# One 512-column matmul for both activation parts in the FFN and output products of a two-layer trunk

## The chip, the core and the metric

The kernel runs on one core of a Trainium2 chip. Its time is the device time of one execution in microseconds (us); the median of three runs is the figure to be predicted.

## What is computed

The reference is a two-layer decoder trunk over 256 tokens of width 2048. What matters here is the second half of each layer and the product that ends the first half:

```python
mod = cond @ ada_w[l] + ada_b[l]                 # 6 vectors of 2048: shift, scale, gate, twice
h = rms_norm(x, norm_mix[l]) * (1.0 + sc1) + sh1
x = x + g1 * hybrid_mixer(h, ...)                # four head groups, concatenated, then y @ w_o
h = rms_norm(x, norm_ffn[l]) * (1.0 + sc2) + sh2
u = causal_dwconv(h @ w_up, conv_w, conv_b)      # width 3; w_up is 2048 x 11264
a, g = split(u); x = x + g2 * ((silu(g) * a) @ w_down)   # w_down is 5632 x 2048
```

All of it is in float32, and the products keep that precision by splitting.

## The kernel before

The sequence lies on the free axis: an activation is a tile of 128 partitions (channels) by 256 tokens, a weight tile of 128x128 is the stationary operand, and a product sums 16 (or more) such tiles into PSUM. Float32 products are made of fast ones: every weight chunk is loaded as float32 (`raw`, 128x1024, 512 KB, `load_w`), ScalarE (ACT) casts it to `hi` (L217), VectorE (DVE) subtracts to get `lo` (L219), and the activations are kept as a pair `act[:, 0]` (high part) and `act[:, 1]` (rest), side by side in SBUF. `products` then gives three matmuls of 256 columns for each weight tile: hi x high, hi x rest, lo x high. The fourth is too small to matter. `raw` has four buffers, `hi` and `lo` three each, so the casts run at most two chunks ahead of TensorE (PE).

`gemm_t` is the product of the FFN and of the output projection. It takes 8 output tiles at a time: a chunk holds one k (128 input channels) and 8 output tiles, and two output tiles share one PSUM bank of 512 float32 columns. The output projection `wo` (L1056 to L1064) runs in two groups of 8 tiles and adds into x (L1061). Its PSUM pool has four banks under the tag `gp`, and `S` (two), `T` and `O` for the attention that runs just before. The last head group, the stick-breaking attention `sb_attn`, computes its eight heads while matmuls of `wo` that need only the other three groups are already possible. The order of instructions on each engine is fixed when the kernel is built, by a scheduler that works from priorities and its own costs.

The FFN works through 44 column tiles of each half of `w_up`: `up(g)` makes 4 of each half at once (11 groups), applies the width-3 convolution (one ACT and two DVE instructions for each tile, L1096 to L1100), SiLU, product and split. `down` multiplies what six (then five) such groups made with `w_down` and adds into x (L1118). The FFN's pool has all eight banks under `gp`. Ahead of it `norm_chunk` makes the 16 activation pairs of h: for each, a DVE multiply (L338), an ACT add (L342) and a DVE subtraction (L343).

The adaLN modulation has a weight matrix of 201 MB in the two layers. It isn't done on PE: a DMA brings 128x1024 pieces (`adaw`, three buffers) and DVE multiplies and sums each (L159, called a dot below, 384 of them). The dots are spread over the program: `tick` adds `rate[0]` to a credit at every weight chunk, and each whole credit emits one job of two dots at a low priority. `RATE[l][i]` sets the rate by layer and phase; phases 3 and 4 are the FFN before and after its first slab.

Of the kernel before, what the change touches and what calls it, by code (L numbers as in the profile page):

```python
# [61 lines left out]
RATE = ((0.45, 0.9, 0.45, 0.45, 0.22), (0.2, 0.2, 0.2, 0.1, 0.1))  # L62
# [10 lines left out]
def tile_trunk(ctx: ExitStack, tc: tile.TileContext, io, out, L):  # L73
# [159 lines left out]
    def gemm_t(pp, chunks, acts, G, tag="gp"):  # L233
# [19 lines left out]
        return ps  # L253

# [739 lines left out]
    for l in range(L):  # L994
# [75 lines left out]
        with ExitStack() as s2:  # L1070
# [14 lines left out]
            def up(g):  # L1085
                ps = gemm_t(pp, [io["wup"][l, g, k] for k in range(KD)], h, 8)
                res = []
                for p in range(2):
                    uu = []
                    for half in range(2):  # L1090
                        src = ps[2 * half + p]
                        u = fp.tile([P, 2, T], F32, tag=f"u{half}", name="u", bufs=2)
                        for q in range(2):
                            i = half * NFF + g * 4 + p * 2 + q
                            w0, w1, w2 = (fw[:, j * 2 * NFF + i:j * 2 * NFF + i + 1] for j in range(3))
                            nc.scalar.activation(u[:, q, :], src[:, q, :], AF.Identity, scale=w2, bias=fb[:, i:i + 1])  # L1096
                            nc.vector.scalar_tensor_tensor(  # L1097
                                u[:, q, 1:], src[:, q, :T - 1], w1, u[:, q, 1:], op0=ALU.mult, op1=ALU.add
                            )
                            nc.vector.scalar_tensor_tensor(  # L1100
                                u[:, q, 2:], src[:, q, :T - 2], w0, u[:, q, 2:], op0=ALU.mult, op1=ALU.add
                            )
                        uu.append(u)
                    sg = fp.tile([P, 2, T], F32, tag="sg", name="sg", bufs=2)
                    last_silu[0] = nc.scalar.activation(sg, uu[1], AF.Silu)
                    nc.vector.tensor_mul(uu[0], uu[0], sg)
                    y_ = fp.tile([P, 2, 2, T], F32R, tag="g", name="g", bufs=14)
                    split(y_, uu[0])
                    res += [y_[:, 0], y_[:, 1]]
                return res  # L1110

            def down(k0, acts, st=None):
                for mg in range(2):
                    ps = gemm_t(pp, [io["wdn"][l, k0 + k, mg] for k in range(len(acts))], acts, 8)
                    for m in range(8):
                        c = mg * 8 + m
                        g2 = mod(l, 5, c | 3)
                        nc.vector.scalar_tensor_tensor(  # L1118
                            x[:, c, :], ps[m // 2][:, m % 2, :], g2[:, c:c + 1], x[:, c, :],
                            op0=ALU.mult, op1=ALU.add,  # L1120
                        )
# [7 lines left out]
            NG = NFF // 4  # L1129
            for g in range(NG):  # L1130
# [4 lines left out]
                if g in (5, NG - 1):  # L1135
# [153 lines left out]
```

## Time and profile before

| | |
|---|---|
| median of 3 runs | 2481.59 us (2481.56 to 2487.34) |
| the profiled execution's own time | 2479.15 us |
| its span in the trace | 2476.8 us |
| PE busy, PE weight loads busy | 97%, 94% of the span |
| DVE busy, ACT busy | 75%, 47% of the span |
| mean granted clock of TensorE | 0.992 |

Busy shares are means over the whole span. Matmuls are pipelined, so the duration of one is longer than the distance from its start to the start of the next, and the latter is what a stream of them costs. In a timeline a row with "x2" is two instructions merged, in brackets stands how long the engine idled just before and what it waited for.

### The profile page before, as it was taken

To read this page: it belongs to the slowest core of one execution; us is meant where nothing else is said; L and a number is where in the kernel's file an instruction comes from. 1 tells how busy PE (TensorE), PEld (TensorE's weight loads), DVE (VectorE), ACT (ScalarE), POOL (GpSimd) and SP (SyncE) were. 2 spreads that over 40 slices of the span, in tenths; PEclk is the share of its full clock that TensorE was granted. 3 is DMA by queue.
4 is the path that set the end of the run, shared out by engine and by line. 5 is a ranking of instruction groups with operands and counts; after the bars stand their busy time and mean duration, and the time that the engine had idled before them with its cause. 6 is when DMAs were issued, how large, how long until landed. Compare 5 with 4: busy or idle time off the path is not lost.

```text
span 2476.8 us, 46041 instructions
## 1 busy us (share of the span) xinstructions
PE 2413.6 (97%) x18720; PEld 2330.1 (94%) x18720; DVE 1853.5 (75%) x2972; ACT 1165.0 (47%) x1704; POOL 24.0 (1%) x40
## 2 busy tenths in 40 slices
PE   7888999999999999999999999999999999999999
PEld 5666999989999999999999999999999999999999
DVE  6779988898888887888767997657676676455554
ACT  2124566445545433445444576644454453344442
POOL 0000000000000000000001000000000000000000
PEclk9999999999999999999999999999999999999999
DMA  8975778988888899888875574366666666655554
GB/s 319 347 256 190 252 271 274 336 300 295 282 307 296 290 331 325 312 304 293 290 259 181 181 242 162 128 222 213 221 207 233 230 207 222 187 176 191 184 182 162
DMA packets 169125, 610.31 MB, mean 246 GB/s; under 512 B 19025, under 2 KB 20945, under 8 KB 168401
## 3 DMA queue, kind: packets, MB, share of 16 engines
q1 hardware_dynamic: 168914, 607.39, 71.1%
q8 instruction: 146, 2.39, 0.4%
q14 instruction: 65, 0.53, 0.1%
HBM read 603.12 MB, written 4.19 MB: 245 GB/s over the span
## 4 chain that ended last, share of the span: by engine, by line
PE 85%; DVE 8%; DMA 4%; ACT 2%; issue 1%; SPq 0%; DVEq 0%; ACTq 0%
PE gt L245 71%; DMA adaw<-in_ada_dram 4%; DVE acc L565 3%; PE gt L359 2%; DVE adaw L159 2%; PE pv L266 2%; PE pn L266 1%; PE s L509 1%; PE po L535 1%; PE pq L266 1%; DVE lo L219 1%; PE tp L530 1%; PE ss L326 1%; ACT hi L217 0%; PE po L981 0%
## 5 line engine op out<-in xcount | busy, mean ns | idle before, releaser
L245 PE MATMUL gt<-act,hi 128*128 128x256 f32 x7232 | 1318.4, 284 | 4.3 <-ACT act L342 4.1
L217 ACT CAST hi<-raw 128x1024 fp32r<-128x1024 f32 (+3 forms) x716 | 739.5, 1033 | 1002.3 <-PE gt L245 831.7
L219 DVE TENSOR_TENSOR lo<-raw,hi 128x1024 fp32r<-128x1024 f32 (+3 forms) x716 | 859.1, 1203 | 388.4 <-ACT hi L217 386.6
L245 PEld LDWEIGHTS gt<-act,hi 128*128 128x128 f32 x7232 | 1129.5, 192 | 7.0 <-ACT act L342 4.9
L245 PE MATMUL gt<-act,lo 128*128 128x256 f32 x3616 | 1021.7, 285 | 3.5 <-DVE lo L219 3.4
L245 PEld LDWEIGHTS gt<-act,lo 128*128 128x128 f32 x3616 | 691.9, 192 | 4.9 <-DVE lo L219 4.7
L159 DVE SCALAR_TENSOR_TENSOR adaw<-adaw,cond 128x1024 f32<-128x1024 f32 x384 | 467.0, 1221 | 126.4 <-DMA adaw<-in_ada_dram 124.3
L245 PE MATMUL gt<-g,hi 128*128 128x256 f32 x2816 | 507.1, 283 | 0.0
L245 PEld LDWEIGHTS gt<-g,hi 128*128 128x128 f32 x2816 | 438.7, 192 | 0.2
L245 PE MATMUL gt<-g,lo 128*128 128x256 f32 x1408 | 396.9, 283 | 0.1
L245 PEld LDWEIGHTS gt<-g,lo 128*128 128x128 f32 x1408 | 269.5, 192 | 0.3 <-DVE lo L219 0.3
L359 PE MATMUL gt<-actw,raw 128*128 128x256 f32 x416 | 106.1, 418 | 26.4 <-ACT actw L340 26.4
L359 PEld LDWEIGHTS gt<-actw,raw 128*128 128x128 f32 x416 | 86.5, 211 | 45.9 <-ACT actw L340 32.3
L565 DVE SCALAR_TENSOR_TENSOR acc<-ug,vec,acc 128x256 f32<-128x256 f32 x240 | 98.9, 476 | 0.0
L1096 ACT ACTIVATE u<-gt,vec 128x256 f32<-128x256 f32 x176 | 94.2, 561 | 5.9 <-PE gt L245 3.4
L1097 DVE SCALAR_TENSOR_TENSOR u<-gt,vec,u 128x255 f32<-128x255 f32 x176 | 79.9, 474 | 3.2 <-ACT u L1096 3.2
L1100 DVE SCALAR_TENSOR_TENSOR u<-gt,vec,u 128x254 f32<-128x254 f32 x176 | 79.4, 472 | 0.0
L359 PE MATMUL gt<-act,hi 128*128 128x256 f32 x416 | 77.1, 287 | 2.1 <-ACT act L342 2.1
L359 PEld LDWEIGHTS gt<-act,hi 128*128 128x128 f32 x416 | 66.1, 195 | 2.5 <-ACT act L342 2.5
L340 ACT ACTIVATE actw<-t,sh 128x256 f32<-128x256 f32 x16 | 8.1, 507 | 121.8 <-DVE sh L414 121.3
L359 PE MATMUL gt<-act,lo 128*128 128x256 f32 x208 | 59.5, 286 | 0.0
L523 ACT ACTIVATE pt<-s,mx,scl 128x128 f32<-128x128 f32 (+1 forms) x96 | 48.4, 512 | 9.7 <-DVE mx L520 9.7
(284 smaller groups left out, 1786.2 us busy)
## 6 DMA issues: line engine op xcount, KB each, us to landing
adaw<-in_ada_dram SPq DMA_DIRECT2D x384, 512.0 KB, 5.5
raw<-in_wup_dram SPq DMA_DIRECT2D x352, 512.0 KB, 4.3
raw<-in_wdn_dram SPq DMA_DIRECT2D x176, 512.0 KB, 4.3
raw<-in_wo_dram SPq DMA_DIRECT2D x64, 512.0 KB, 4.7
raw<-in_wconv_dram SPq DMA_DIRECT2D x32, 512.0 KB, 5.5
raw<-in_wsqk_dram SPq DMA_DIRECT2D x32, 512.0 KB, 4.3
raw<-in_wlq_dram SPq DMA_DIRECT2D x32, 448.0 KB, 4.7
raw<-in_wnkv_dram SPq DMA_DIRECT2D x32, 412.0 KB, 3.1
```

The source lines that it names most:

```text
L159: nc.vector.scalar_tensor_tensor(w, w, 1.0, cond[:, hf * 1024:hf * 1024 + 1024], op0=ALU.mult, op1=ALU.mult, accum_out=raw[:, hf, j:j + 1],)
L217: nc.scalar.copy(hi[:, :n], raw[:, :n])
L219: nc.vector.tensor_sub(lo[:, :n], raw[:, :n], hi[:, :n].bitcast(F32))
L245: nc.tensor.matmul(ps[m // 2][:, m % 2, :], ww[:, c], x, start=(k == 0 and i == 0 and m % 2 == 0), stop=(k == K - 1 and i == len(prods) - ...
L266: nc.tensor.matmul(o, x[:, tt * P:(tt + 1) * P], ww[:, kk * N + c0:kk * N + c1], start=(k == 0 and i == 0 and first), stop=(k == K - 1 and ...
L326: nc.tensor.matmul(self.ss[:, 0, :], ones, sq[:, q, :], start=(self.n == 2 and q == 0), stop=(self.n == KD and q == 1 - join))
L359: nc.tensor.matmul(ps[m // 2][:, m % 2, :], ww[:, m * P:(m + 1) * P], xx, start=(first and i == 0 and m % 2 == 0), stop=(last and i == len ...
L523: nc.scalar.activation(pt[:, j, :n], s[:, j, :n], AF.Exp, scale=sc2[:, j:j + 1], bias=mx[:, j:j + 1], accum_out=rs[:, tt, 2 * pr + j:2 * p ...
L565: nc.vector.scalar_tensor_tensor(acc[:, c, :], ug[:, c, j:j + T], w, acc[:, c, :], op0=ALU.mult, op1=ALU.add)
L1096: nc.scalar.activation(u[:, q, :], src[:, q, :], AF.Identity, scale=w2, bias=fb[:, i:i + 1])
L1097: nc.vector.scalar_tensor_tensor(u[:, q, 1:], src[:, q, :T - 1], w1, u[:, q, 1:], op0=ALU.mult, op1=ALU.add)
L1100: nc.vector.scalar_tensor_tensor(u[:, q, 2:], src[:, q, :T - 2], w0, u[:, q, 2:], op0=ALU.mult, op1=ALU.add)
```

## The change

- A new `gemm_2` takes 4 output tiles at a time, each with a whole bank. For each k and tile it issues two matmuls: `hi` against both activation parts in one matmul of 512 columns (high part into the bank's first half, rest into its second), and `lo` against the high part, 256 columns, added into the second half. The three products that are summed stay the same.
- The halves of a bank are summed later. In `up` an ACT copy takes the second half to SBUF (`v`) and a DVE addition adds the first. In `down` and `wo` the multiply-add into x is done twice, once for each half.
- A chunk holds two k by 4 tiles instead of one k by 8. The number and size of the loads stay. `up` runs 22 groups instead of 11, `down` and `wo` 4 groups of output tiles instead of 2; in `wo` every second group takes the banks O, T, S and one gp.
- The FFN's rates of dots are now 0.2 in `up` and 0.42 in `down` in layer 0 (0.45 before and 0.22 after the first slab), 0.1 in both in layer 1 (as before).

```diff
-RATE = ((0.45, 0.9, 0.45, 0.45, 0.22), (0.2, 0.2, 0.2, 0.1, 0.1))
+RATE = ((0.45, 0.9, 0.45), (0.2, 0.2, 0.2))
+RATE_FFN = ((0.2, 0.42), (0.1, 0.1))
+    def gemm_2(banks, chunks, acts):
+        K, G = len(acts), len(banks)
+        k = 0
+        for src in chunks:
+            hi, lo = load_w(src)
+            for kk in range(src.shape[-1] // (G * P)):
+                x2 = acts[k].rearrange("p a t -> p (a t)")
+                for m in range(G):
+                    c = slice((kk * G + m) * P, (kk * G + m + 1) * P)
+                    nc.tensor.matmul(
+                        banks[m].rearrange("p a t -> p (a t)"), hi[:, c], x2,
+                        start=(k == 0), stop=False, skip_group_check=True,
+                    )
+                    nc.tensor.matmul(
+                        banks[m][:, 1, :], lo[:, c], acts[k][:, 0, :],
+                        start=False, stop=(k == K - 1), skip_group_check=True,
+                    )
+                k += 1
...
-        for mg in range(2):
-            ps = gemm_t(pp, [io["wo"][l, mg, k] for k in range(KD)], y, 8)
-            for m in range(8):
-                c = mg * 8 + m
+        for mg in range(4):
+            ps = [pp.tile([P, 2, T], F32, tag=t, name="gt") for t in (("gp",) * 4 if mg % 2 == 0 else ("O", "T", "S", "gp"))]
+            gemm_2(ps, [io["wo"][l, mg, k] for k in range(KD // 2)], y)
+            for m in range(4):
+                c = mg * 4 + m
                 g1 = mod(l, 2, c | 3)
-                nc.vector.scalar_tensor_tensor(
-                    x[:, c, :], ps[m // 2][:, m % 2, :], g1[:, c:c + 1], x[:, c, :], op0=ALU.mult, op1=ALU.add
-                )
+                for q in range(2):
+                    nc.vector.scalar_tensor_tensor(
+                        x[:, c, :], ps[m][:, q, :], g1[:, c:c + 1], x[:, c, :], op0=ALU.mult, op1=ALU.add
+                    )
...
+                        v = fp.tile([P, T], F32, tag="v", name="v", bufs=2)
+                        nc.scalar.copy(v, src[:, 1, :])
+                        nc.vector.tensor_add(v, src[:, 0, :], v)
```

The scheduler places everything anew. Three places matter below.

**TensorE at the end of the attention of layer 0.** `po` is the attention's output, `ss` sums the squares for the norm of this last head group, act_3463 is its first normed activation tile, and `gt` are the products of `wo`. Before:

```order
L982 MATMUL po_3381<-sa_3446,sv_2834 128x128
L245 MATMUL gt_3480<-act_3305,hi_3722 128x256 x2
...
L445 MATMUL ss_3453<-sq_3451,ones_73 128x256 x4
L245 MATMUL gt_3478<-act_3273,hi_3752 128x256 x2
L245 MATMUL gt_3478<-act_3273,lo_3754 128x256
L245 MATMUL gt_3479<-act_3273,hi_3752 128x256 x2
...
L245 MATMUL gt_3478<-act_3463,hi_3884 128x256 x2
```

Now:

```order
L1002 MATMUL z_3433<-ssp_3441,con_69 128x128
L1003 MATMUL z_3433<-ssp_3441,negones_75 128x128
L1006 MATMUL po_3381<-sa_3446,sv_2834 128x256
L1007 MATMUL po_3381<-sa_3446,sv_2834 128x128
L269 MATMUL gt_3702<-act_1553,hi_3708 128x512
L273 MATMUL gt_3702<-act_1553,lo_3710 128x256
L269 MATMUL gt_3702<-act_1553,hi_3708 128x512
L273 MATMUL gt_3702<-act_1553,lo_3710 128x256
L470 MATMUL ss_3453<-sq_3451,ones_73 128x256 x4
L269 MATMUL gt_3478<-act_3463,hi_3638 128x512
```

Before, 15 `gt` matmuls stood between `po` and `ss`, and 93 between `ss` and the first that reads act_3463 (165 in layer 1). Now four stand between `po` and `ss`, none behind `ss` (five and three in layer 1), and none between the last z and its `po`.

**VectorE at the start of the FFN of layer 1.** t1 and act are the two steps of `norm_chunk`, `lo` is a weight chunk's rest. Before, each further `lo` stood after two more chunks of h, and a chunk of weights served one k:

```order
L219 TENSOR_TENSOR lo_18692<-raw_18688,hi_18690 128x1024
L338 SCALAR_TENSOR_TENSOR t1_18557<-x_17469,amul_18547,actw_18536 128x256
...
L159 SCALAR_TENSOR_TENSOR adaw_18810,modr1_5_18290<-adaw_18810,cond_85 128x1024
...
L219 TENSOR_TENSOR lo_18722<-raw_18718,hi_18720 128x1024
L343 SCALAR_TENSOR_TENSOR act_18551<-t1_18582,mod1_3_11213,act_18551 128x256
```

Here lo_18692 is the third `lo` of the FFN and lo_18722 the fourth. Now:

```order
L222 TENSOR_TENSOR lo_16420<-raw_16416,hi_16418 128x1024
L368 SCALAR_TENSOR_TENSOR act_16274<-t1_16283,mod1_3_11155,act_16274 128x256
...
L363 SCALAR_TENSOR_TENSOR t1_16295<-x_15429,amul_16273,actw_16262 128x256
L161 SCALAR_TENSOR_TENSOR adaw_16357,modr1_4_11152<-adaw_16357,cond_85 128x1024
L368 SCALAR_TENSOR_TENSOR act_16275<-t1_16291,mod1_3_11155,act_16275 128x256
...
L363 SCALAR_TENSOR_TENSOR t1_16329<-x_15429,amul_16273,actw_16262 128x256
L1105 SCALAR_TENSOR_TENSOR amul_16273<-mod1_4_11154,vs1_7429 128x4
L178 TENSOR_TENSOR mod1_3_11155<-modr1_3_11153 128x4
L222 TENSOR_TENSOR lo_16442<-raw_16438,hi_16440 128x1024
L368 SCALAR_TENSOR_TENSOR act_16279<-t1_16325,mod1_3_11155,act_16279 128x256
```

lo_16420 is the second `lo` of this FFN (k = 2 and 3) and lo_16442 the third (k = 4 and 5). It stands behind the first ten chunks of h, with a dot in each of the four pairs of chunks after the first.

**VectorE at the start of the FFN of layer 0.** Before, the fourth `lo` stood behind the sixth chunk of h:

```order
L159 SCALAR_TENSOR_TENSOR adaw_4405,modr0_4_2227<-adaw_4405,cond_85 128x1024
L343 SCALAR_TENSOR_TENSOR act_4600<-t1_4624,mod0_3_2230,act_4600 128x256
...
L338 SCALAR_TENSOR_TENSOR t1_4636<-x_3475,amul_4597,actw_4586 128x256
L219 TENSOR_TENSOR lo_4814<-raw_4810,hi_4812 128x1024
```

Now the fourth, lo_4552 (k = 6 and 7), stands behind twelve chunks with one dot in each pair, and two more dots (three stand ahead of the fifth):

```order
L161 SCALAR_TENSOR_TENSOR adaw_4437,modr0_4_2227<-adaw_4437,cond_85 128x1024
L368 SCALAR_TENSOR_TENSOR act_4371<-t1_4417,mod0_3_2230,act_4371 128x256
L368 SCALAR_TENSOR_TENSOR act_4371<-t1_4421,mod0_3_2230,act_4371 128x256
L161 SCALAR_TENSOR_TENSOR adaw_4440,modr0_4_2227<-adaw_4440,cond_85 128x1024
L161 SCALAR_TENSOR_TENSOR adaw_4446,modr0_3_2228<-adaw_4446,cond_85 128x1024
L178 TENSOR_TENSOR mod0_4_2229<-modr0_4_2227 128x4
L222 TENSOR_TENSOR lo_4552<-raw_4548,hi_4550 128x1024
```

Over the program 143 of the 384 `adaw` loads were issued ahead of the FFN of layer 0 (now 145), 176 within it (now 156: 55 in the first 104 loads of `up`, 35 in the first `down`, 34 in the rest of `up`, 32 in the last `down`, which had 23), and 28 in the FFN of layer 1 (now 41).

## Rows read from the trace of the kernel before

**Rows 1.** The page: the span, and the engines' busy time.

```profile
span 2476.8 us, 46041 instructions
PE 2413.6 (97%) x18720; PEld 2330.1 (94%) x18720; DVE 1853.5 (75%) x2972; ACT 1165.0 (47%) x1704; POOL 24.0 (1%) x40
```

**Rows 2.** Busy time by stretch: in layer 0 the FFN's first seven groups of `up`, the rest of `up`, and the last `down`; in layer 1 the first `down`. Columns are the stretch, its length, busy time (instructions) of PE, weight loads, DVE, ACT and POOL, granted clock, DMA share, GB/s.

```profile
520.00:842.00 322.00, 319.89 (x2652) 319.48 (x2651) 276.74 (x416) 159.08 (x196) 0.00 (x0) 0.99 0.84 294
990.00:1174.00 184.00, 184.00 (x1536) 184.00 (x1535) 155.77 (x228) 89.59 (x108) 0.00 (x0) 1.00 0.86 304
1174.00:1290.00 116.00, 114.32 (x930) 112.85 (x929) 86.13 (x122) 49.30 (x55) 0.20 (x1) 1.00 0.79 279
2032.00:2170.00 138.00, 138.00 (x1152) 138.00 (x1151) 77.35 (x90) 56.25 (x61) 0.00 (x0) 1.00 0.63 206
```

**Rows 3.** The page: the weight loads of the three products by count and size.

```profile
raw<-in_wup_dram SPq DMA_DIRECT2D x352, 512.0 KB, 4.3
raw<-in_wdn_dram SPq DMA_DIRECT2D x176, 512.0 KB, 4.3
raw<-in_wo_dram SPq DMA_DIRECT2D x64, 512.0 KB, 4.7
```

**Rows 4.** Groups by shape, DVE and ACT: count, busy us, mean ns of one, idle before.

```profile
L1097 DVE SCALAR_TENSOR_TENSOR u<-gt,vec,u 128x255 f32<-128x255 f32 x176 | 79.9, 474 | 3.2 <-ACT u L1096 3.2
L1118 DVE SCALAR_TENSOR_TENSOR x<-gt,mod,x 128x256 f32<-128x256 f32 x64 | 26.0, 476 | 11.4 <-PE gt L245 11.4
L324 DVE TENSOR_TENSOR sq<-sq 128x256 f32<-128x256 f32 x12 | 5.1, 423 | 0.0
L532 ACT COPY pT<-tp 128x256 f32<-128x256 f32 x24 | 8.9, 372 | 3.4 <-PE tp L530 2.3 <-PE po L535 1.0
```

**Rows 5.** Timeline of PE in `up` of layer 1: start us, duration us, instruction. Between these two rows lies one merged row of two matmuls.

```profile
1802.00 0.28 PE L245 MATMUL gt<-act,lo 128*128 128x256 f32 x1
...
1802.36 0.28 PE L245 MATMUL gt<-act,lo 128*128 128x256 f32 x1
```

**Rows 6.** Timeline of PE, wider products of the same split kind: 412 columns, then 512.

```profile
1400.71 0.91 PE L266 MATMUL pn<-hi,act 128*128 128x412 f32 x4
1401.46 0.54 PE L266 MATMUL pn<-lo,act 128*128 128x412 f32 x2
1401.83 0.91 PE L266 MATMUL pn<-hi,act 128*128 128x412 f32 x4
...
1429.25 0.39 PE L266 MATMUL pk<-hi,latn 128*128 128x512 f32 x1
1429.47 0.39 PE L266 MATMUL pk<-lo,latn 128*128 128x512 f32 x1
1429.70 0.61 PE L266 MATMUL pk<-hi,latn 128*128 128x512 f32 x2
```

**Rows 7.** Timelines at the end of the attention of layer 0: ACT takes `po` out, PE sums the squares and goes on with `wo`, DVE scales and splits the last head group.

```profile
435.44 0.59 ACT L983 COPY osb<-po 128x512 f32<-128x512 f32 x1 [1.01 <-PE po L982]
...
437.17 1.99 PE L445 MATMUL ss<-sq,ones 128*128 128x256 f32 x8
438.81 0.59 PE L245 MATMUL gt<-act,hi 128*128 128x256 f32 x2
...
440.16 1.67 DVE L453 SCALAR_TENSOR_TENSOR osb<-osb,vec,r 128x256 f32<-128x256 f32 x4 [0.48 <-ACT r L288]
441.75 0.68 DVE L283 TENSOR_TENSOR act<-osb,act 128x512 fp32r<-128x512 f32 x1
```

**Rows 8.** Timelines at the start of the FFN of layer 0: DVE, and the first matmul of `up`.

```profile
514.84 0.88 DVE L338 SCALAR_TENSOR_TENSOR t<-x,amul,actw 128x256 f32<-128x256 f32 x2 [0.69 <-ACT actw L288]
515.64 1.22 DVE L219 TENSOR_TENSOR lo<-raw,hi 128x1024 fp32r<-128x1024 f32 x1
516.78 0.87 DVE L343 SCALAR_TENSOR_TENSOR act<-t,mod,act 128x256 fp32r<-128x256 f32 x2
517.57 0.87 DVE L338 SCALAR_TENSOR_TENSOR t<-x,amul,actw 128x256 f32<-128x256 f32 x2
518.36 1.22 DVE L159 SCALAR_TENSOR_TENSOR adaw<-adaw,cond 128x1024 f32<-128x1024 f32 x1
519.50 0.08 DVE L159 DVE_READ_ACCUMULATOR adaw<-adaw,cond 128x1 f32 x1
...
515.92 1.22 PE L245 MATMUL gt<-act,hi 128*128 128x256 f32 x4 [2.07 <-ACT act L342]
```

**Rows 9.** The same place in layer 1.

```profile
1710.54 0.88 DVE L338 SCALAR_TENSOR_TENSOR t<-x,amul,actw 128x256 f32<-128x256 f32 x2 [1.34 <-ACT actw L288]
...
1711.62 0.91 PE L245 MATMUL gt<-act,hi 128*128 128x256 f32 x5 [2.07 <-ACT act L342]
```

**Rows 10.** Timelines at the end of the kernel: the last matmul, and DVE's additions of the last 8 tiles into x.

```profile
2471.96 0.28 PE L245 MATMUL gt<-g,lo 128*128 128x256 f32 x1
...
2470.12 3.23 DVE L1118 SCALAR_TENSOR_TENSOR x<-gt,mod,x 128x256 f32<-128x256 f32 x8 [4.30 <-PE gt L245]
```

**Rows 11.** Busy time by stretch around the idle time ahead of the FFN of layer 0 (columns as in rows 2).

```profile
514.00:516.00 2.00, 0.08 (x1) 0.08 (x1) 1.30 (x4) 1.42 (x4) 0.00 (x0) 0.97 0.97 371
516.00:518.00 2.00, 1.83 (x7) 1.54 (x8) 2.00 (x5) 0.27 (x1) 0.00 (x0) 0.50 0.98 391
522.00:526.00 4.00, 4.00 (x36) 4.00 (x35) 3.94 (x10) 2.48 (x5) 0.00 (x0) 1.00 0.79 310
```

More of the change, by code (lines that the diff above doesn't have):

```diff
@@ L193, in phase @@
     def phase(l, i):
-        rate[0] = RATE[l][i]
+        if i < 3:
+            rate[0] = RATE[l][i]
         gate[0] = GATE[l][i]
@@ L1085, in up @@
             def up(g):
[L1086 to L1092, printed above, removed]
+                rate[0] = RATE_FFN[l][0]
+                ps = [pp.tile([P, 2, T], F32, tag="gp", name="gt") for _ in range(4)]
@@ new lines, in up @@
+                gemm_2(ps, [io["wup"][l, g, k] for k in range(KD // 2)], h)
+                uu = []
+                for half in range(2):
+                    u = fp.tile([P, 2, T], F32, tag=f"u{half}", name="u", bufs=2)
+                    for q in range(2):
+                        src = ps[2 * half + q]
+                        v = fp.tile([P, T], F32, tag="v", name="v", bufs=2)
+                        nc.scalar.copy(v, src[:, 1, :])
+                        nc.vector.tensor_add(v, src[:, 0, :], v)
+                        i = half * NFF + g * 2 + q
+                        w0, w1, w2 = (fw[:, j * 2 * NFF + i:j * 2 * NFF + i + 1] for j in range(3))
+                        nc.scalar.activation(u[:, q, :], v, AF.Identity, scale=w2, bias=fb[:, i:i + 1])
+                        nc.vector.scalar_tensor_tensor(
+                            u[:, q, 1:], v[:, :T - 1], w1, u[:, q, 1:], op0=ALU.mult, op1=ALU.add
+                        )
+                        nc.vector.scalar_tensor_tensor(
+                            u[:, q, 2:], v[:, :T - 2], w0, u[:, q, 2:], op0=ALU.mult, op1=ALU.add
+                        )
+                    uu.append(u)
@@ new lines, in up, with down @@
+                sg = fp.tile([P, 2, T], F32, tag="sg", name="sg", bufs=2)
+                last_silu[0] = nc.scalar.activation(sg, uu[1], AF.Silu)
+                nc.vector.tensor_mul(uu[0], uu[0], sg)
+                y_ = fp.tile([P, 2, 2, T], F32R, tag="g", name="g", bufs=14)
+                split(y_, uu[0])
+                return [y_[:, 0], y_[:, 1]]
+            def down(k0, acts, st=None):
+                rate[0] = RATE_FFN[l][1]
+                for mg in range(4):
+                    ps = [pp.tile([P, 2, T], F32, tag="gp", name="gt") for _ in range(4)]
+                    gemm_2(ps, [io["wdn"][l, mg, k0 // 2 + k] for k in range(len(acts) // 2)], acts)
+                    for m in range(4):
+                        c = mg * 4 + m
+                        g2 = mod(l, 5, c | 3)
@@ L1100, in up @@
[L1100 to L1121, printed above, removed]
+                                x[:, c, :], ps[m][:, q, :], g2[:, c:c + 1], x[:, c, :],
@@ L1122, in down @@
+                                op0=ALU.mult, op1=ALU.add,
+                            )
                         if st and m % 2:
@@ L1128, in tile_trunk @@
             k0 = 0
-            NG = NFF // 4
+            NG = NFF // 2
             for g in range(NG):
@@ L1134, in tile_trunk @@
                     pend = None
-                if g in (5, NG - 1):
+                if g in (11, NG - 1):
                     pend = (k0, slab)
```

16 lines of the change are left out of this document (7 added, 9 removed).

## The prediction

> **What bounds the kernel now.** I read the page first: PE is busy for 2413.6 of 2476.8 us and its weight loads for nearly as long [rows 1]. Then the stretches, since a share of the whole says little: in the second stretch of `up` in layer 0 PE is busy for 184.00 of 184.00 us, with DVE at 155.77 and ACT at 89.59, and in layer 1's first `down` for 138.00 of 138.00 [rows 2]. So in the FFN the end is set by how fast PE can take matmuls, and DVE is the engine next to it, in layer 0 above all. The timeline gives PE's price: from one `lo` matmul to the next 0.36 us pass, for three matmuls of 256 columns [rows 5]. That is 120 ns each; at 2.4 GHz the 256 columns themselves take 106.7 ns, so 13 ns come on top of each matmul, with a fresh weight tile each time.
>
> **What PE saves.** A weight tile meets a pair in two matmuls, 512 and 256 columns. The 256 stay at 120 ns. For the 512 the trace has rows: two in 0.45 us (225 ns, 12 above the 213.3 of the columns), and 412 columns take 1.12/6 = 187 ns, 15 above their 171.7 [rows 6]. So the surplus doesn't grow with the columns, and I take 227 ns. A pair costs 347 instead of 360 ns. The three products have 352 + 176 + 64 loads [rows 3] of 8 tiles each, 4736 pairs, so 4736 x 13 ns = **62 us less**. With the surplus of 15 or 12 ns on the wide one alone, the bounds are 12 x 4736 = 57 and 15 x 4736 = 71 us. A load then holds PE for 8 x 0.347 = 2.78 us, instead of 2.88.
>
> The Trainium skill, "TensorE: Matmul & The Clock Gate", section "Back-to-back issue gap", speaks against this: it gives the gap as columns / 2.4 + 2.5 ns, by which 256 columns take 109 ns and a dropped matmul saves 2.5 ns, 12 us in all. This trace disagrees, with 120 ns at 256 columns; the sum above goes by the rows.
>
> **What is added.** For each `up` tile one ACT copy (372 ns by the nearest row) and one DVE addition (423 ns), for each tile of `down` and `wo` a second multiply-add of 476 ns [rows 4]. ACT is at half load everywhere and hides its part. On DVE, 16 loads of `up` hold 8 tiles, so 8 x 0.42 / 16 = 0.21 us more per load; the dots in layer 0 fall from 74 in 112 loads to 55 in 104, 0.13 x 1.22 = 0.16 us less (the dot as in [rows 8]). The stretch before held 276.74 us in 112 loads, 2.47 each [rows 2], so now 2.52 of 2.78 us, 91% where it was 86%. PE idled for only 2.1 us of that stretch, so DVE's load alone is no bound; the cover is the two chunks that `hi` and `lo` lead. The last `down` of layer 0 is tighter: 86.13 us [rows 2] + 9 more dots (11.0) + 16 multiply-adds (7.6) = 104.7 in 40 x 2.78 = 111 us, 94%. For these two I take **5 us** of waits, from 0 to 39 (see the rivals).
>
> **What is moved.** Here the rebuilt order costs PE. I count only what the order of instructions forces, with the trace's durations.
>
> *End of the attention, each layer.* Before, 93 matmuls behind `ss` (11 us) covered the norm and the split of the last head group. From ACT's copy of `po` at 435.44 to the end of the split at 441.75 + 0.68 = 442.43 it takes 7.0 us [rows 7]. None of it gets shorter, and both parts are needed at once by the wide matmul. PE has two pairs (0.7) and the sums (438.81 - 437.17 = 1.64) to do in it, so it idles for some 4.7 us in layer 0, in layer 1 (with four pairs) some 4. Add 0.8 for the last head without filler (one ACT exponential and its hand-overs, twice 0.4 as in ACT's copy rows [rows 4]), and in layer 0 the next `lo` of `wo` behind three dots and a split, about 1 us late. I take 7.5 + 5 = **12.5 us**.
>
> *Start of the FFN.* The group is half as wide, so PE wants a new k every 1.39 us instead of 2.88, while DVE has to make h at its old pace: 0.80 (two t1) + 0.79 (two act), with a dot of 1.14 us 2.73 us for two k, from start to start [rows 8]. Worse, `lo` now comes late. Layer 0: lo_4552 is done at 514.84 + 6 x 2.73 + 2 x 1.14 + 1.14 = 534.6. PE has done k = 0 to 5 by 514.84 + 3 x 2.73 + 2.78 = 525.8, and waits 8.8 us. The remaining ten k take 13.9 us, to 548.5, and the second group 22.2, to 570.7. Before, the same work took 46.1 us from 515.92 [rows 8] and 3.3 us of waits and slow clock, to 565.3. It ends 5.4 us later where 128 pairs should have saved 1.7, so 7 us go. Layer 1: lo_16442 is done at 1710.54 + 5 x 2.73 + 0.80 + 1.14 = 1726.1; PE has had k = 0 to 3 by 1718.8 and waits 7.3 us; the groups end at 1726.1 + 6 x 2.78 + 22.2 = 1765.0. Before, they ended at 1711.62 + 46.1 = 1757.7 [rows 9]. So 7.3 + 1.7 = 9 us go. Together **16 us**; with the dots late for their DMA up to 22, with the first pair of h ready earlier 12.
>
> *The last additions of a phase.* Eight multiply-adds of 0.40 us follow the last matmuls of `wo` and `down`. Before, the 8 tiles came 0.36 us apart, and the last addition ended at 2473.35, 1.1 us behind the last matmul's end at 2472.24 [rows 10]. Now 4 tiles come 0.35 us apart and the 8 additions take 3.2 us from the first, which is ready about 0.6 us before PE's end: 2.6 us behind it. Four such places (`wo` twice, the last `down` twice), 1.5 us each: **6 us**, 4 to 8.
>
> *The clock.* After PE's idle of 2.07 us before 515.92 [rows 8] the granted clock was 0.50 in the next stretch and 1.00 four us later [rows 11]: 1.2 instead of 2.4 GHz. The new idle times are longer, so I add **3 us**, 0 to 7.
>
> Sum: -62 + 5 + 12.5 + 16 + 6 + 3 = **-19 us** against the profiled execution's 2479.15, so 2460. The median lies 2.4 us above that execution, and I predict **2463 us**. Moving dots out of layer 0's FFN to layer 1 costs nothing: there DVE is busy for 77.35 of 138 us [rows 2].
>
> **Rivals.**
> 1. *Most of the gain stays* (0.13): the waits at the attention's end and the FFN's starts don't come, as PE is late anyway and the waits ahead of them make up for one another. For it: in the trace before, nearly no wait of that kind reaches PE. Against: the order is fixed, and the forced waits rest on durations alone. Then -62 + 6 + 5 and some 5 of the rest: 2436.
> 2. *DVE becomes the bound in layer 0's FFN, slower* (0.22). If DVE's idle time there isn't slack but hand-overs that stay, each load keeps (322 - 276.74)/112 = 0.40 us of it: 2.92 us against PE's 2.78, 15 us over 104 loads, and in the last `down` 104.7 + 29.9 - 111 = 24. That is 39 instead of my 5, and the time is 2497. It decides against the change as soon as 24 of the 39 are real. For it: 94% of busy time with DMA queues that must then carry more, too. Against: PE without idle time beside a DVE at 85% [rows 2].
> 3. *No gain on PE* (0.05): a wide matmul costs twice a narrow one, 240 ns. Against: 225 ns [rows 6]. Then only the losses are left, 2524. By the page named above it would be about 2512.
>
> My forecast itself has 0.60 and lies between 2450 and 2476, by the bounds of its terms.
>
> **From there to the numbers.** A difference of less than 0.3% (7.4 us) is none that a measurement of this kernel can tell. Faster: nearly all of the forecast, rival 1, and a little of rival 2: 0.73. Within: 0.13, from rival 2 and the forecast's upper end. Slower: 0.14, the rest of rival 2 and rival 3. The range takes in half of rival 1 and more than half of rival 2: 2440 to 2488.
>
> **What would show it.** Steps of 0.347 us from one `lo` matmul to the next in both FFNs. PE idle for 4 us or more behind `ss` in both attentions, and 7 to 9 us within the first eight k of each FFN, put down to `lo`. PE still without idle time in the rest of `up` and the first `down`. The prediction is wrong if the wide matmul takes clearly more or less than 227 ns, if PE waits for `lo` all through layer 0's FFN, or if the two starts pass without those waits.

## The result and the profile after

The changed kernel takes 2510.38 us (median of 4, 2498.98 to 2514.49), the kernel before on the same chip 2483.76 (2481.56 to 2487.34): 1.0101 times as long, 95% interval 1.0073 to 1.0128. It is **slower by 1%**; forecast were 2463 us and faster, in a range up to 2488. The profiled execution took 2508.87 us.

The page after, to be read beside [rows 1]; then the wide and the narrow matmuls, and the adaLN dots (count, busy us, mean ns, idle time before):

```profile
span 2507.0 us, 37134 instructions
PE 2393.1 (95%) x13984; PEld 2082.6 (83%) x13984; DVE 1952.2 (78%) x3244; ACT 1227.2 (49%) x1880; POOL 25.2 (1%) x40
...
L269 PE MATMUL gt<-act,hi 128*128 128x512 f32 x3328 | 1185.9, 401 | 16.3 <-DVE act L368 7.4
...
L273 PE MATMUL gt<-act,lo 128*128 128x256 f32 x3328 | 942.5, 284 | 20.0 <-DVE lo L222 19.7
...
L161 DVE SCALAR_TENSOR_TENSOR adaw<-adaw,cond 128x1024 f32<-128x1024 f32 x384 | 466.6, 1222 | 139.3 <-DMA adaw<-in_ada_dram 138.0
```

A quarter of PE's instructions is gone, and PE is busy for only 20 us less. Most of its waits for `lo` are new: 26.5 us in all (19.7 in the row above, 6.7 in `down`), 3.4 before. The stretches, with the columns of [rows 2]:

```profile
549.00:842.00 293.00, 293.00 (x1661) 254.22 (x1660) 252.27 (x390) 168.01 (x235) 0.00 (x0) 1.00 0.79 268
842.00:990.00 148.00, 140.99 (x794) 121.02 (x793) 116.20 (x169) 52.64 (x50) 0.20 (x1) 1.00 0.88 306
990.00:1174.00 184.00, 176.68 (x994) 153.41 (x993) 150.94 (x236) 100.62 (x142) 0.00 (x0) 0.98 0.75 254
1174.00:1310.00 136.00, 129.16 (x722) 111.74 (x721) 114.75 (x176) 56.85 (x63) 0.00 (x0) 0.99 0.89 314
1735.00:1770.00 35.00, 22.97 (x93) 18.89 (x94) 31.57 (x66) 15.90 (x27) 0.00 (x0) 0.71 0.66 239
2050.00:2190.00 140.00, 140.00 (x794) 121.42 (x793) 91.49 (x122) 55.59 (x58) 0.00 (x0) 1.00 0.68 222
```

PE waits in layer 0 from the first `down` on (842 to 1310) and around the start of layer 1's FFN (1735 to 1770). Layer 1's FFN has no idle time after that, and yet it gives little: 794 matmuls in 140 us are 397 pairs of 353 ns, where 347 were forecast.

Here is the change stage by stage, between the starts of the first or last matmuls of each in the two profiled executions (us). The forecast is that of the prediction's terms, with 13 ns for each pair of the stage:

```
stage                                        before   after   change   forecast
start, to the first pq matmul                 219.4   214.8    -4.6       0
attention and wo of layer 0                   296.5   309.6   +13.1     +5.7
FFN of layer 0                                768.4   781.4   +13.0    -15.5
from there to the first up of layer 1         427.3   440.2   +12.9     +4.7
FFN of layer 1                                760.4   755.2    -5.2    -18.5
end                                             4.8     5.8    +1.0     +1.5
```

The first stage is the same code in both and ended anywhere from 214.8 to 225.0 us in the profiled executions below, so lengths of stages are compared, not moments. The clock's 3 us are not spread over the stages.

### The profile page after: what moved, and what is told of

It reads as the page before. It is cut to its first block, busy times and chain, and to the rows that moved or that the text cites. A ratio compares the mean times of both kernels' runs of the same rounds, so it can differ in the third digit from the quotient of the medians.

```text
span 2507.0 us, 37134 instructions
## 1 busy us (share of the span) xinstructions
PE 2393.1 (95%) x13984; PEld 2082.6 (83%) x13984; DVE 1952.2 (78%) x3244; ACT 1227.2 (49%) x1880; POOL 25.2 (1%) x40
## 4 chain that ended last, share of the span: by engine, by line
PE 76%; DVE 11%; DMA 9%; ACT 3%; issue 1%; SPq 0%; DVEq 0%; ACTq 0%
PE gt L269 38%; PE gt L273 20%; DMA adaw<-in_ada_dram 8%; PE gt L384 3%; DVE adaw L161 3%; PE gt L248 3%; DVE lo L222 3%; DVE acc L590 2%; PE pv L291 2%; PE pn L291 1%; PE s L534 1%; PE po L560 1%; PE pq L291 1%; DVE x L1150 1%; PE ss L351 1%
## 5 line engine op out<-in xcount | busy, mean ns | idle before, releaser
L269 PE MATMUL gt<-act,hi 128*128 128x512 f32 x3328 | 1185.9, 401 | 16.3 <-DVE act L368 7.4
L222 DVE TENSOR_TENSOR lo<-raw,hi 128x1024 fp32r<-128x1024 f32 (+3 forms) x716 | 858.2, 1203 | 309.5 <-ACT hi L220 304.0
L273 PE MATMUL gt<-act,lo 128*128 128x256 f32 x3328 | 942.5, 284 | 20.0 <-DVE lo L222 19.7
L269 PEld LDWEIGHTS gt<-act,hi 128*128 128x128 f32 x3328 | 630.6, 190 | 171.1 <-DVE act L368 8.5
L273 PEld LDWEIGHTS gt<-act,lo 128*128 128x128 f32 x3328 | 634.4, 191 | 24.8 <-DVE lo L222 24.2
L269 PE MATMUL gt<-g,hi 128*128 128x512 f32 x1408 | 496.6, 397 | 2.4 <-DVE x L1150 2.4
L269 PEld LDWEIGHTS gt<-g,hi 128*128 128x128 f32 x1408 | 264.7, 188 | 65.6 <-issue 2.7
L248 PE MATMUL gt<-act,hi 128*128 128x256 f32 x576 | 113.7, 291 | 0.0
L1126 ACT ACTIVATE u<-v,vec 128x256 f32<-128x256 f32 x176 | 97.3, 597 | 17.1 <-DVE v L1123 12.4
L1122 ACT COPY v<-gt 128x256 f32<-128x256 f32 x176 | 64.2, 371 | 64.6 <-PE gt L273 36.4
L248 PEld LDWEIGHTS gt<-act,hi 128*128 128x128 f32 x576 | 91.0, 191 | 1.1
L1127 DVE SCALAR_TENSOR_TENSOR u<-v,vec,u 128x255 f32<-128x255 f32 x176 | 80.0, 479 | 9.3 <-ACT u L1126 9.3
L1130 DVE SCALAR_TENSOR_TENSOR u<-v,vec,u 128x254 f32<-128x254 f32 x176 | 79.9, 479 | 1.8
L384 PE MATMUL gt<-act,hi 128*128 128x256 f32 x416 | 77.1, 287 | 2.1 <-ACT act L367 2.1
```

Of the source, the lines that this page charges most:

```text
L222: nc.vector.tensor_sub(lo[:, :n], raw[:, :n], hi[:, :n].bitcast(F32))
L248: nc.tensor.matmul(ps[m // 2][:, m % 2, :], ww[:, c], x, start=(k == 0 and i == 0 and m % 2 == 0), stop=(k == K - 1 and i == len(prods) - ...
L269: nc.tensor.matmul(banks[m].rearrange("p a t -> p (a t)"), hi[:, c], x2, start=(k == 0), stop=False, skip_group_check=True,)
L273: nc.tensor.matmul(banks[m][:, 1, :], lo[:, c], acts[k][:, 0, :], start=False, stop=(k == K - 1), skip_group_check=True,)
L384: nc.tensor.matmul(ps[m // 2][:, m % 2, :], ww[:, m * P:(m + 1) * P], xx, start=(first and i == 0 and m % 2 == 0), stop=(last and i == len ...
L1126: nc.scalar.activation(u[:, q, :], v, AF.Identity, scale=w2, bias=fb[:, i:i + 1])
```

## Experiments

The kernel before was run beside each; ratios are to it, with 95% intervals.

**1. What a pair costs, without other engines.** All loops are replaced by matmuls on resident tiles; the change's order, for example, as

```diff
+for m in range(4):
+    wide(ps, m, cs[m], k0, False)
+    nar(ps, m, cs[m], False, k1)
```

> Only TensorE work on tiles that are already in SBUF, nothing of the reference is computed. Nine stretches of six bursts, 12 k by 4 tiles each; a burst starts after a short wait on an ACT copy, as a load of the kernel would after a late chunk. Stretches in this order: 512 with fresh weights only; wide then narrow on each tile, as the change has it; the narrow one into the other half of the bank; narrow before wide; four wide then four narrow; two and two; the narrow one a tile behind; three matmuls of 256 (as before the change); the change's order again. In the changed kernel a pair takes 346.7 ns after some waits and 353.3 ns (three pairs in 1060 ns) after others, and stays at it until the next wait. Theory: the 353 ns belong to the alternation of a wide and a narrow matmul itself and start or not by the moment at which the stretch begins; then the change's order shows both paces here too, without any other engine at work, triples are always at 360, and some other order shows 346.7 in all its bursts. Rival: the slower pace comes from traffic of DVE, ACT and the DMA queues beside PE; then every burst here is at 346.7 whatever the order.

Measured, from start to start, ns for one tile (a wide and a narrow matmul):

```
change's order, both stretches       353.3 in 12 of 12 bursts
narrow one into the other half       353.3 in 6 of 6
narrow one a tile behind             353.3 in 6 of 6
narrow before wide                   353.3 and 346.7 by turns, 3 bursts each
four wide, four narrow               350.0
two and two                          348.3
three matmuls of 256 columns         360.0
two matmuls of 512 columns           453.3
```

PE is alone here, so the rival is out: the slower pace is PE's own, for this alternation. The theory missed in two points: the change's order showed the slower pace only, and no order was at 346.7 in all its bursts. Behind the first burst none began with a wait, and the next run sees to that. Three pairs in a row look like this in the changed kernel, first in layer 0's `up`, then in its first `down` (start us, duration us, instruction):

```profile
700.23 0.28 PE L273 MATMUL gt<-act,lo 128*128 128x256 f32 x1
700.35 0.40 PE L269 MATMUL gt<-act,hi 128*128 128x512 f32 x1
700.58 0.28 PE L273 MATMUL gt<-act,lo 128*128 128x256 f32 x1
700.70 0.40 PE L269 MATMUL gt<-act,hi 128*128 128x512 f32 x1
700.93 0.28 PE L273 MATMUL gt<-act,lo 128*128 128x256 f32 x1
701.04 0.40 PE L269 MATMUL gt<-act,hi 128*128 128x512 f32 x1
701.28 0.28 PE L273 MATMUL gt<-act,lo 128*128 128x256 f32 x1
...
900.07 0.28 PE L273 MATMUL gt<-g,lo 128*128 128x256 f32 x1
...
900.42 0.28 PE L273 MATMUL gt<-g,lo 128*128 128x256 f32 x1
...
900.76 0.28 PE L273 MATMUL gt<-g,lo 128*128 128x256 f32 x1
...
901.11 0.28 PE L273 MATMUL gt<-g,lo 128*128 128x256 f32 x1
```

From `lo` to `lo` the first takes 0.35, 0.35, 0.35 and 1.05 to 1.06 in all (1060 ns in the unrounded starts), the second 1.04. The mean of a wide matmul in the first is 236 ns, not 227.

**2. The same, from real waits.** As above, with the last weight tile rewritten ahead of each burst.

> Again only TensorE work on resident tiles, nothing of the reference. In the first such run the bursts followed each other without a wait: the change's order stayed at 353.3 ns in all its bursts, narrow before wide went from 353.3 to 346.7 and back each time two matmuls of one kind stood side by side, two and two gave 348.3 and four and four 350.0. Here each burst begins with a real wait, for the last weight tile of hi or of lo, of a length that differs from burst to burst. Stretches of eight bursts: change's order (warming up), the same behind hi, behind lo, two and two, four and four, eight and eight behind hi, eight and eight behind lo, the change's order again. Theory: a wait restarts the pattern at another moment, so the change's order shows both 346.7 and 353.3 among its bursts, and the orders in blocks stay between (348 to 351) whatever the wait. Rival: from rest the change's order always falls into one of the two, and the mixture in the kernel has another cause; then all 24 of its bursts are alike.

The change's order (24 bursts after the warming ones): 19 at 346.7, 5 at 353.3, each at one pace throughout. Two and two: 348.3 in all 8; four and four: 350.0 to 350.8; eight and eight: 349.2 in all 16, where the wait was hidden behind the narrow ones. So the pace is mostly settled when PE starts again, and it is the alternation that has two of them; the blocks have one. Not every change of pace needs a wait: in the changed kernel PE went from 353.3 to 346.7 at 833 us, in run 8 from 346.7 to 353.3 at 678 us, between matmuls that show no idle time. What in PE makes the two was not found.

**3. The output product as before.** `wo` in groups of eight tiles of 256-column matmuls, with the weights' old layout:

```diff
-        for mg in range(4):
-            gemm_2(ps, [io["wo"][l, mg, k] for k in range(KD // 2)], y)
+        for mg in range(2):
+            ps = gemm_t(pp, [io["wo"][l, mg, k] for k in range(KD)], y, 8)
```

> The changed kernel with the output product alone put back to groups of eight tiles in matmuls of 256 columns, and the old layout of its weights. Theory: the narrow groups there cost more than they give: the ends of both attentions are 3.7 to 4.8 us of PE waits behind ss and some 4 more of small ones, and the last additions come later, while 512 pairs give only 512 x (7 to 13) ns = 3.6 to 6.7 us; so 12 to 20 us faster than the changed kernel, 2490 to 2498, and the PE wait behind ss is gone in both layers. Rival: the waits only move, since the start of the FFN is behind the norm in either form; then 2505 to 2512.

2493.36 us, ratio 1.002 (0.999 to 1.005): 17 us less than the changed kernel. From the first pq to the FFN, layer 0 takes 298.9 us instead of 309.6, and from layer 0's FFN to layer 1's it is 432.2 instead of 440.2. Layer 1's FFN takes 749.1 instead of 755.2, but some 4 us of that are pace: 545 steps of its first `up` are at 346.7, where the changed kernel has 353.3. PE's waits from 380 to 441 us, of the changed kernel and then of this one (us in total, times, longest):

```profile
PE gt L269 <- DVE act L308: 3.3, 1, 3.3
PE z L1001 <- DVE ssp L1000: 3.1, 3, 1.3
PE po L1006 <- ACT sa L1005: 1.5, 3, 0.6
PE gt L269 <- ACT osb L1008: 0.7, 1, 0.7
```

```profile
PE z L1001 <- DVE ssp L1000: 1.4, 2, 0.7
```

The wait behind `ss` is gone, in layer 1 as well, and so are 3.2 of the 4.6 us of waits in the last heads, which had lost the matmuls that filled them. The theory holds in place and size.

**4. The rates alone.** The kernel before with `RATE_FFN = ((0.2, 0.42), (0.1, 0.1))`, set in `up` and `down`; its matmuls unchanged.

> The kernel before with the change's rates of the adaLN dots in the FFN alone (0.2 in up, 0.42 in down), all matmuls as before. Theory: layer 0's down then waits for lo behind dots whose DMA is late, as in the changed kernel, so 5 to 15 us slower than before, 2488 to 2498, with PE idle in 842 to 1290 us and DVE waiting there for adaw. Rival: the waits of the changed kernel come from its second multiply-add per tile and the half-wide groups on DVE; then the rates alone cost less than 3 us, or give some by freeing up's DVE.

2505.14 us, ratio 1.0082 (1.0064 to 1.01): **20 us slower**. The theory had the sign, but put it at 15 us at most. Of 28 us in the profiled execution 7.9 lie in layer 0's FFN, where PE now waits 4.9 us for `lo` and 1.8 for `sq`; 10.5 lie between the two FFNs and 8.7 in layer 1's FFN. Those stand around its start. The dots on DVE from 1705 to 1760 us, in the kernel before and in this one:

```profile
L159 DVE SCALAR_TENSOR_TENSOR adaw<-adaw,cond 128x1024 f32<-128x1024 f32 x4 | 4.9, 1218 | 0.4 <-DMA adaw<-in_ada_dram 0.4
```

```profile
L160 DVE SCALAR_TENSOR_TENSOR adaw<-adaw,cond 128x1024 f32<-128x1024 f32 x15 | 18.2, 1221 | 2.8 <-DMA adaw<-in_ada_dram 2.8
```

The norm ahead of layer 1's FFN needs that layer's second scale and shift. With fewer dots behind it these were not finished, and the rest ran on DVE between the norm's steps. From 1690 to 1770 us PE waits 11.5 us here, for the sums of squares, h and `lo`, where it waited 2.1 before.

**5. Layer 0's `down` without the dots' transfers.** In `ada_dot`, while a `down` of layer 0 is issued:

```diff
+            if here[0]:
+                ch = cond[:, hf * 1024:hf * 1024 + 1024]
+                nc.vector.scalar_tensor_tensor(
+                    w, ch, 1e-5, ch, op0=ALU.mult, op1=ALU.mult, accum_out=raw[:, hf, j:j + 1],
+                )
+                continue
```

> The changed kernel; the dots that fall into layer 0's two downs (some 36) multiply cond with itself, with the same time on DVE and no transfer (what they should give is left out). Theory: PE's 21 us of waits in layer 0's downs and the up between are DVE waiting for the dots' transfers, with lo queued behind the waiting dot; without the transfers at least 12 us go, 2490 to 2498, with less than 4 us of PE idle time in each of the two downs. Rival: DVE's own load makes lo late (its multiply-adds and dots together); then less than 5 us go, and the waits for lo stay.

2493.30 us, ratio 1.0031 (1.0001 to 1.0061), 17 us less than the changed kernel. The stretch from 845 to 970 us, in the changed kernel and here:

```profile
845.00:970.00 125.00, 118.29 (x667) 101.51 (x666) 95.37 (x138) 44.21 (x42) 0.20 (x1) 1.00 0.88 304
```

```profile
845.00:970.00 125.00, 125.00 (x709) 108.33 (x709) 107.17 (x160) 48.20 (x47) 0.20 (x1) 1.00 0.66 197
```

DVE does more here and PE never waits: it isn't DVE's load alone. In the changed kernel DVE stands for 29.5 us of this stretch in front of dots whose data is not there, and PE for 6.7 behind the `lo` queued there:

```profile
DVE adaw L161 <- DMA adaw<-in_ada_dram: 29.5, 20, 2.8
...
PE gt L273 <- DVE lo L222: 6.7, 8, 1.2
```

The doubled additions have a part in it: five of the eight waits come right behind a dot that had waited for its data, the other three (3.6 us) behind the eight additions, with such dots just ahead of them. One of these, on DVE:

```profile
935.90 1.22 DVE L161 SCALAR_TENSOR_TENSOR adaw<-adaw,cond 128x1024 f32<-128x1024 f32 x1 [1.86 <-DMA adaw<-in_ada_dram]
...
938.19 3.22 DVE L1150 SCALAR_TENSOR_TENSOR x<-gt,mod,x 128x256 f32<-128x256 f32 x8
941.32 2.35 DVE L222 TENSOR_TENSOR lo<-raw,hi 128x1024 fp32r<-128x1024 f32 x2
```

Layer 0's FFN takes 766.9 instead of 781.4 us. Its first `down` falls from 143.0 to 135.6, the `up` behind it from 212.7 to 204.8; the last `down` keeps 120.8 of 121.7, with 6.3 us of waits for the sums of squares where less than 4 were expected. But the 17 us have chance in them: this execution had 2085 steps of layer 1's FFN at 346.7 ns, and that stage took 741.0 instead of 755.2 us, with nothing changed in it; the stages ahead of layer 0's FFN took 8.9 us more.

**6. Layer 1's rates up.** `RATE` of layer 1 from (0.2, 0.2, 0.2) to (0.3, 0.3, 0.35).

> The changed kernel with layer 1's rates of the dots outside the FFN at 0.3, 0.3, 0.35 instead of 0.2. In the changed kernel 337 of the 384 dots stand ahead of 1705 us, 356 in the kernel before, and the norm ahead of layer 1's FFN needs 352: 15 dots then run in the 55 us around that norm instead of 4. Theory: the dots that the change took out of layer 0's FFN are late there and hold up norm and lo, so with the higher rates PE's waits between the output product's end and the second group of up shrink by 10 to 17 us and the kernel comes to 2493 to 2500. Rival: the start of layer 1's FFN is slow because the half-wide groups need h twice as early, whatever the dots do; then less than 4 us go.

2495.57 us, ratio 1.0059 (1.0037 to 1.0082), but 2492.1 to 2509.7 one by one. By stages it is less than hoped: 438.9 us between the FFNs instead of 440.2, and 749.0 in layer 1's FFN instead of 755.2, all of it in the first `up` (296.7 instead of 302.9) and at the same pace. The dots from 1705 to 1760 us are 9 instead of 16, PE's waits from 1715 to 1770 fall from the first three lines to the second three:

```profile
PE gt L273 <- DVE lo L222: 4.8, 1, 4.8
PE ss L351 <- ACT sq L345: 4.5, 1, 4.5
PE gt L269 <- DVE act L368: 3.5, 1, 3.5
```

```profile
PE gt L269 <- DVE act L368: 2.8, 1, 2.8
PE ss L351 <- ACT sq L345: 2.2, 2, 1.7
PE gt L269 <- DVE x L1088: 0.5, 1, 0.5
```

So the late dots make some 7.5 us in the changed kernel (1.3 + 6.2), less than the 10 expected. Putting `wo` back (run 3) took 8 us out of the same place.

**7. Eight wide, then eight narrow ones.** In `gemm_2`, the inner loops over both k and four tiles run once for hi and then once for lo.

> The changed kernel; within a load all eight wide matmuls go first, then the eight narrow ones, so that lo may be 1.9 us later than hi. Theory: a pair takes 350 ns throughout, where the changed kernel has 353.3 for two thirds of its pairs and 346.7 for the others, which leaves the sum nearly alone (0 to -8 us), and PE's waits for lo in layer 0's downs (some 20 us) halve at least: 2488 to 2500. Rival: the waits for lo come from a late transfer that delays DVE by more than 1.9 us each time, and the next hi behind it; then they come back on hi, and the time stays within 2503 to 2512.

2509.09 us, ratio 1.0106 (1.0084 to 1.0129): no gain, the rival's time. Waits for `lo` in layer 0 fall from 14.2 to 9.2 us, but one of 6.7 for `sq` comes in the last `down`. By stages the profiled execution gains 3.0 us in layer 0's FFN and 11.0 in layer 1's; it loses 6.0 up to the first pq, in code that is the same, 4.4 from there to the FFN and 2.2 between the FFNs. The four executions lie within 5 us (2508.2 to 2512.9).

**8. The old rates in the changed kernel.** `RATE` as before the change, no `RATE_FFN`.

> The changed kernel with the rates of the dots as they were before (0.45 in layer 0's first up, 0.22 in the rest of its FFN; layer 1 alike), all matmuls as changed. The rates alone made the kernel before 20 us slower. Theory: with the wide matmuls they cost about as much, so the changed kernel gets back 10 to 20 us, to 2490 to 2500: its downs in layer 0 wait less than 2 us each, the start of layer 1's FFN loses its late dots, and the first up of layer 0 gives a few us back, since DVE there has 0.2 us more work per load. Rival: the first up of layer 0 becomes DVE's, with 252 us of work for 293 now and 14 more dots in it (17 us) next to more multiply-adds, and takes 10 us or more longer; then 2503 to 2515.

2503.50 us, ratio 1.0077 (1.0058 to 1.0097): 7 us less, between the two; the intervals overlap, so that the 7 us alone are not clear of the noise. Layer 0's first `up` grows from 303.7 to 309.5 us, its first `down` falls from 143.0 to 138.9. In that `up` PE now waits, with DVE at 95% and the transfers at 0.91:

```profile
560.00:800.00 240.00, 236.54 (x1345) 205.32 (x1344) 226.89 (x368) 135.12 (x190) 0.00 (x0) 1.00 0.91 316
```

Thus at neither rate did layer 0's FFN gain by the wide matmuls: it takes 780.7 us here, 781.4 in the changed kernel and 768.4 before. What the old rates give back lies at the start of layer 1's FFN: 2.2 us between the FFNs and 6.4 in the FFN. Without the rates the wide matmuls cost 19 us, the rates without them 20, both together 27.

**9. Four things at once.** Output product as before, eight and eight, layer 1's rates as in 6, and 0.25 in `up` and 0.32 in `down` in layer 0.

> The changed kernel with the output product as before, eight wide matmuls first within a load of the FFN, layer 1's rates at 0.3, 0.3, 0.35, and 0.25 in up and 0.32 in down in layer 0. Theory: the losses are separate (17 us for the output product, 10 to 17 at layer 1's FFN start, 10 for layer 0's waits), so they add up to 35 to 45 us and the kernel lands at 2465 to 2475, faster than before by 0.4 to 0.8%. Rival: they cover for one another, since DVE and the transfers stay as loaded as they were; then 2480 to 2490, the same as before.

2482.63 us, ratio 0.9994 (0.998 to 1.0009): the same as before, the rival. Layer 1's FFN takes 737.4 us, 23 less than before the change, layer 0's 783.4, 15 more.

**10. Wide matmuls where DVE has room.** The kernel before with `gemm_2` in layer 1's FFN alone, eight and eight, old rates:

```diff
+            up, down = (up2, down2) if l else (up1, down1)
```

> The kernel before with the wide matmuls in layer 1's FFN alone, eight wide and then eight narrow ones per load; all else, rates too, as before. Theory: where DVE has room the wide matmul gives what PE's price says: 2112 pairs x (360 - 349.2) = 23 us, less 3 to 7 at the start of that FFN, where h is wanted twice as early, and 1 to 2 at the end: 2465 to 2472, faster by 0.5 to 0.8%. Rival: the start and the end take more, as in the changed kernel, whose layer 1 FFN gave 5 us only; then 2478 to 2485.

**2463.36 us**, ratio 0.9922 (0.9906 to 0.9939): faster than both kernels. Layer 1's FFN takes 737.4 instead of 760.4 us, and its first `up`, with the start, 290.5 us, which is 832 pairs of 349.2: no loss at the start at all. That loss was put at 3 to 7 us.

**11. Layer 0's `down` too.**

```diff
-            up, down = (up2, down2) if l else (up1, down1)
+            up, down = up2 if l else up1, down2
```

> As the run with layer 1's FFN alone, and in layer 0 the two downs in wide matmuls too (its ups and both output products as before). Theory: at the old rates layer 0's downs have room for a second multiply-add per tile, and 704 pairs x 10.8 = 7.6 us go, less 1 to 3 at the sum of squares in the last down: 4 to 7 us below the run with layer 1's FFN alone. Rival: in the last down of layer 0 the eight multiply-adds, the dots and lo queue up on DVE, and PE waits as long as in the changed kernel; then it is 0 to 6 us above that run.

2464.85 us, ratio 0.9927 (0.9907 to 0.9948): the same as run 10, where 4 to 7 us less were expected. Beside run 10 the first `down` of layer 0 falls from 139.5 to 134.0 us, the last grows from 117.5 to 120.5, where the sums of squares wait for the doubled additions:

```profile
PE ss L348 <- DVE sq L346: 2.5, 1, 2.5
PE ss L348 <- ACT sq L342: 2.5, 2, 2.1
PE gt L265 <- DVE x L1183: 0.6, 1, 0.6
```

**12. Run 10 in the change's order.** Here a wide one and its narrow one go by turns.

> As the run with wide matmuls in layer 1's FFN alone (2463.4 us), but in the change's own order, a wide one and its narrow one on each tile. Theory: nothing waits in that FFN after its start, so the pace that it falls into there, 346.7 or 353.3 ns a pair, holds for nearly all 2112 pairs, 14 us apart: the executions form two groups, near 2458 and near 2472, and the profiled one has one pace in at least 1900 pairs. Rival: the pace changes often within an execution and evens out; then all executions lie within 2460 to 2468, with both paces in the trace.

2463.92 us, ratio 0.9919 (0.9898 to 0.994). The executions: 2459.7, 2460.1, 2461.8, 2466.0, 2472.8, 2472.9, three and two of them some 12 us apart, and one between. The profiled one (2460.14) has 346.7 ns in all but a few of its pairs. A stretch of layer 1's second `up`, of the changed kernel, of run 10 and of this one:

```profile
2190.00:2390.00 200.00, 200.00 (x1135) 173.34 (x1134) 133.88 (x187) 111.27 (x155) 0.00 (x0) 1.00 0.63 188
```

```profile
2136.00:2336.00 200.00, 200.00 (x1146) 175.91 (x1146) 136.91 (x191) 109.20 (x152) 0.00 (x0) 1.00 0.60 189
```

```profile
2140.00:2340.00 200.00, 200.00 (x1156) 176.34 (x1155) 137.47 (x193) 111.04 (x152) 0.00 (x0) 1.00 0.58 190
```

PE is never idle in any of the three, and does 1135, 1146 and 1156 matmuls. Only profiled executions show the pace, so that it makes the two groups of times fits them, but isn't shown.

## Why the prediction was wrong

The prediction said 2463 us, 19 less than before; it was 2510, 27 more. Two steps of it failed: the price of a pair, and the dots that were to cost nothing in their new place. Three sizes were too small: the waits in layer 0's FFN, the output product and the clock.

- **What PE saves: mis-sized, 62 us forecast, some 40 there.** Layer 1's FFN ran at 353.3 ns in 2084 of its 2112 pairs, and 2112 x (353.3 - 347) = 13.3 us is just what it lacks of its forecast (-5.2 instead of -18.5). Over all three products, steps of three pairs in 1060 ns stand against those in 1040 like 3227 to 1182: 351.5 ns on average, 8.5 x 4736 = 40 us less than 360. The step that failed is adding the price of a 512 between equals [rows 6] to that of a 256 between equals [rows 5]. Both are right by themselves (453.3 / 2 and 120.0 ns in run 1), and their sum, 346.7, comes at one pace only. The bounds 57 to 71 held no doubt on that. The rule of the Trainium skill, "TensorE: Matmul & The Clock Gate", section "Back-to-back issue gap", has columns / 2.4 + 2.5 ns for the gap of an isolated matmul; an estimate by it is 215.8 + 109.2 = 325 ns for the pair. Both paces are above that.
- **"Moving dots out of layer 0's FFN to layer 1 costs nothing": wrong.** The rates alone made the kernel before 20 us slower (run 4). In the changed kernel the late dots make some 7.5 us at the start of layer 1's FFN (run 6), and the old rates 8.6 there (run 8). I looked at DVE's share in layer 1's FFN, where the dots have room, and not at when that layer's norm needs their results. No rival named it.
- **Waits in layer 0's FFN: 5 us forecast, 21 there** (14.2 for `lo`, 6.8 for additions and squares). Rival 2 (39 us, 24 of them enough to decide against the change) had the sign, but of the 21 us only 6.8 lie in the last `down`, where it saw 24, and none in the first `up` beyond its start, where it saw 15. Nor had it the mechanism: DVE is not full, it stands in front of dots whose transfers are late, and the doubled additions and `lo` behind it (run 5). Its mention of the queues, "that must then carry more, too", was the point. The cover of two chunks was taken as enough because PE idled little before, when DVE waited for dots for only 12.3 us from 842 to 990, not 31.6.
- **End of the attention: right place, half the size.** The wait behind `ss` came nearly as forecast: 3.3 + 0.7 us in layer 0 and 2.9 + 0.2 in layer 1, for 4.7 and 4. The last heads of layer 0 wait for 4.6 us (3.1 + 1.5), 1.1 before, where 0.8 was given. The forecast's terms for layer 0 are 4.7 + 0.8 + 1 = 6.5, not the 7.5 that it took. Putting `wo` back gave 17 us, where its terms add up to 12.5 + 3 - 6.7 = 9.
- **Start of the FFN: 16 us forecast, some 13 came, the cause in part.** The first `up` took 9.8 us (layer 0) and 9.0 us (layer 1) more than its 832 pairs of 353.3; before, it took 5.8 and 0 more than its 896 tiles of 360, so 4.0 and 9.0 are new, for 7 and 9. PE waited 6.6 and 4.8 us for `lo`, where 8.8 and 7.3 were forecast. With fewer dots at that place the loss in layer 1 is 2.8 (run 6: 296.7 - 293.9), and with the old `wo` as well 2.6 in the change's order (run 12: 291.0 - 288.4) and nothing in blocks (run 10). So in layer 1 it was for the most part the dots, not the groups of half the width.
- **Last additions:** 1.0 us at the kernel's end, 1.5 forecast. **Clock:** the mean granted clock fell from 0.992 to 0.984, some 40 us more at 1.2 instead of 2.4 GHz. In all stretches at 0.50 together PE was busy for 62.6 us, 32.5 before, and a pair takes 640 ns there instead of some 350. By these the clock's price is about 30 x 290 / 640 = 14 us, not 3, in part counted in the start of the FFN. The longest such stretch, where PE was busy for 60% of the time:

```profile
1736.70:1750.40 13.70, 8.17 (x21) 6.28 (x22) 10.91 (x22) 6.53 (x12) 0.00 (x0) 0.50 0.80 276
```

Open are what in PE makes the two paces, and a full account of layer 0's FFN. It missed its forecast by 28.5 us: 16 are the waits beyond the 5 forecast and some 7 the pace (350.3 ns on average), and the rest wasn't taken apart. The 17 (`wo`), 17 (transfers) and 7 us (old rates) of single runs can't be added up, since the pace of layer 1's FFN alone moves a run by up to 14.

## What to carry to other kernels

Price a mix of instructions from a mix: two forms that each have a clean price may have another by turns, and even two of them. Work that is moved in time has a due date as well as a price: look at who reads its result, not only at whether the new place has room. And a saving on the bounding engine is real only where the next one, with the transfers that it waits for, has slack for its share: wide matmuls gave 23 us in layer 1's FFN at the old rates (run 10), and with the change layer 0's FFN lost 13.

## What was not expected of the hardware

A 512- and a 256-column matmul by turns, each with its own weights, run at 346.7 or at 353.3 ns a pair with nothing else at work. Whichever it is can last for the whole of an FFN, 2084 pairs at the slower in the changed kernel's layer 1, 2085 at the faster in run 5's, which is the same code, and most changes come at a wait; two without one are named in run 2. In blocks of two, four or eight the pair has one price (348.3, 350.0 to 350.8, 349.2). For this FFN alone that is 755.2 or 741.0 us.
